# adaLN weights requested ahead of their sums, and differential attention's transposes one stage later, in a decoder block on one core

## The chip, the cores and the metric

The kernel runs on one core of one Trainium2 chip. A core has a matmul engine (TensorE, PE in the profile), three engines for elementwise work (VectorE or DVE, ScalarE or ACT, GpSimd or POOL), a sequencer that issues transfers (SyncE, SP), and 16 DMA engines that bring data from HBM into the core's memory. Matmul results land in eight banks of a separate memory (PSUM), from which DVE and ACT read them. The engines run side by side and wait for one another through semaphores; each works through its own instructions in the order in which they stand in its queue. The metric is the time of one execution on the device, in microseconds (us), as the median of several runs.

## The reference

One decoder block is computed for 512 tokens of width 1024 (cut to what matters here):

```python
mod = jnp.dot(jax.nn.silu(c), w_ada) + b_ada             # w_ada: 1024 x 6144
sh1, sc1, g1, sh2, sc2, g2 = jnp.split(mod, 6, axis=-1)
h = rmsnorm(x, norm_mix) * (1.0 + sc1) + sh1
rq, rk, rv, rg, dq, dk, dv, gate_r, gate_d = jnp.split(jnp.dot(h, w_in), ...)
ro = head_rms(retention(rope(rq), rope(rk), rv)) * jax.nn.silu(rg)      # 4 heads
# differential attention, 4 heads, two softmax maps each, query blocks of 128, causal:
s = jnp.einsum('bqhcd,bkhcd->bhcqk', qi, k) * scale      # c = 0, 1
p = jax.nn.softmax(jnp.where(kpos <= qpos, s, neg), axis=-1)
a = p[:, :, 0] - lam * p[:, :, 1]
o = jnp.einsum('bhqk,bkhe->bqhe', a, v)
do = head_rms(o) * diff_norm * (1.0 - lambda_init)
merged = sigmoid(gate_r) * (ro @ w_ret_o) + sigmoid(gate_d) * (do @ w_diff_o)
x = x + g1 * (merged @ w_out)
y = hierarchical_moe(rmsnorm(x, norm_ffn) * (1.0 + sc2) + sh2, ...)     # 32 experts, 2 per token
x = x + g2 * y;  return rmsnorm(x, norm_final)
```

Only sh1 and sc1 are needed at the start. g1, sh2, sc2 and g2 (four rows of 1024 numbers, each from a slice of w_ada of 1024 x 1024) are needed only behind the mixer.

## The kernel before

**The products that fill TensorE.** The mixer is a sequence of large products of the 512 normalised tokens with slices of 512 columns of `w_in`, `w_ret_o`, `w_diff_o` and `w_out`. Weights arrive in tiles `wst`; ACT rounds each to `whi` (line 179), DVE computes the rest `wlo` (line 180), and each product is three matmuls: high by high, high by low, low by high (`products`, line 225, results in a pool of PSUM banks called `pj`). After every three matmuls `products` calls `tick`, which lets every side job in the list `lanes` advance to its next `yield`. So a side job's instructions stand on PE's queue between product matmuls, and the number of yields between two of its steps says how many threes of product matmuls stand between them. PE's order is the order in which the code is written (`manual_schedule`); on DVE, ACT, POOL and SP a scheduler sets the order when the program is built.

**Side job `ada_rows` (lines 467 to 492).** For each of the four later rows it asks for eight tiles `wa2` of w_ada, 128 x 1024 numbers (512 KB) each (line 474), multiplies each by one column of silu(c) and adds it to `acc` on DVE (lines 476 and 478), yields 6 times after each and 14 times after the last, and then lets PE sum `acc` over the partitions (line 485). `wa2` has two buffers.

**Side job differential attention (`DiffHead`, lines 705 to 760).** It runs in two lanes, each of two heads of four query blocks: eight blocks j = 0 to 7 a lane. The steps of a block are

- `scores` (PE line 724), twice (c = 0, 1), each in a PSUM bank of its own; then on DVE the mask (725), the row maximum (727) and its scaling (728); on ACT the exponential with the row sum (731); on DVE the division and the difference of the two maps (737, 738). A block's scores are 128 x 128, x 256, x 384 or x 512, by the number of keys that its queries see.
- `turn_probs`: PE transposes the probabilities (746), ACT and DVE split them into `aT` and `aTl` (495, 496).
- `values`: PE multiplies them by v (501); ACT squares and sums (535), DVE and POOL make the reciprocal root (536, 537), and DVE scales the result into `od` (757).
- `turn`: two transposes of `od` on PE (572), which ACT and DVE split into `xhi` and `xlo` for the later product with `w_diff_o` (495, 496).

In the text, S(j), Pr(j), V(j) and T(j) are these four steps of block j on PE. `pipelined` (line 576) writes them out: for each block j first T(j-1), then S(j+1), 2 yields, Pr(j), 4 yields, V(j), 4 yields. Retention's heads go through the same function with other numbers.

**The banks.** S (two), Pr, T and V each take a tile of the PSUM pool `pm`, called `ps`, which has three banks and hands them out in turn. A step that writes a bank waits until the step three tiles earlier has been read out.

Of the kernel before, what the change touches and what calls it, by code (L numbers as in the profile page):

```python
# [7 lines left out]
F32 = mybir.dt.float32  # L8
# [5 lines left out]
ALU = mybir.AluOpType  # L14
# [4 lines left out]
P = 128  # L19
D = 1024  # L20
S = 512
KD = D // P
# [19 lines left out]
SIDE_AT = 2, 4, 4, 5  # L42
SIDES = [[(j // 2, j % 2, i) for j in range(4) if SIDE_AT[j] == k for i in range(NT)] for k in range(KD)]
UNITS = [0, 1, 4, 9, 2, 5, 10, 3, 6, 11, 7, 8, 12]
ADA_STEP, ADA_WAIT = 6, 14
RET_WAITS = (4, (2, 5), 2), (3, (4, 6), 2)
DIFF_WAITS = (5, (2, 4, 4), 3), (5, (2, 4, 4), 0)
START_STEPS = (1, 2, 2, 2, 1)
# [85 lines left out]
def block_kernel(tc, a, out):  # L134
    nc = tc.nc
    vec, act, pe, pool = nc.vector, nc.scalar, nc.tensor, nc.gpsimd

    def left(name, bufs=1):
        return open_pool(tc, name, bufs, side="left", reuse_waits="tile")
# [31 lines left out]
    def small(name, cols, dt=F32, p=cp, bufs=None):  # L171
        return p.tile([P, cols], dt, name=name, bufs=bufs)
# [34 lines left out]
    def drain(lane):  # L207
        while lane in lanes:
            tick()
# [21 lines left out]
    def group(pieces, dhi, dlo, transposed, needs=None, kps=()):  # L231

        kps = load_group(pieces, kps)
        banks = new_banks()
        for kp in range(4):
            if kp == 3:
                drain(needs)
            for b in range(4):
                products(banks[b], b, kp, kps[kp], dhi, dlo, transposed)
        return banks  # L240
# [25 lines left out]
    sT = small("sT", KD)  # L266
# [188 lines left out]
    lp, lp_close = left("ada2")  # L455

    def rope(ps, name):
        sw = qk.tile([P, S], F32, name="sw", bufs=2)
        act.copy(sw[0:64, :], ps[64:128, :])
        act.copy(sw[64:128, :], ps[0:64, :])  # L460
        o = qk.tile([P, S], F32, name="qk", bufs=8)
        vec.tensor_mul(o, ps, cosT)
        pool.tensor_mul(sw, sw, sinT)
        vec.tensor_add(o, o, sw)
        return o

    def ada_rows():

        for s_ in range(4):
            lo_col = (2 + s_) * D  # L470
            acc = lp.tile([P, D], F32, name="acc")
            for k in range(KD):
                wa = lp.tile([P, D], F32, name="wa2", bufs=2)
                nc.sync.dma_start(wa, a["w_ada"][0, k * P:(k + 1) * P, lo_col:lo_col + D])
                if k == 0:
                    vec.tensor_scalar(acc, wa, sT[:, 0:1], None, op0=ALU.mult)
                else:
                    vec.scalar_tensor_tensor(acc, wa, sT[:, k:k + 1], acc, op0=ALU.mult, op1=ALU.add)  # L478
                for _ in range(ADA_STEP):
                    yield  # L480
            for _ in range(ADA_WAIT):
                yield
            ps = pm.tile([P, S], F32, name="ps")
            for j in range(4):
                pe.matmul(ps[32 * j:32 * j + 1, 0:256], ones, acc[:, j * 256:(j + 1) * 256], start=True, stop=True)
            brow = lp.tile([P, D], F32, name="wa2", bufs=2)[0:1]
            nc.sync.dma_start(brow, a["b_ada"][:, lo_col:lo_col + D])
            for j in range(4):
                bj = brow[:, j * 256:(j + 1) * 256]
                vec.tensor_add(bj, ps[32 * j:32 * j + 1, 0:256], bj)  # L490
            nc.sync.dma_start(modrow[s_:s_ + 1, :], brow)
            yield

    def split_out(hi, lo, src):
        act.copy(hi, src)
        vec.tensor_sub(lo, src, hi.bitcast(F32))  # L496
# [76 lines left out]
        split_out(hi[:, 2 * h:2 * h + 2, i * P:(i + 1) * P], lo[:, 2 * h:2 * h + 2, i * P:(i + 1) * P],  # L573
                  pt[:, 0:256].rearrange("p (j t) -> p j t", j=2))

    def pipelined(heads, stages, lead, waits, tail):

        blocks = [(head, i) for head in heads for i in range(NT)]
        blocks[0][0].scores(0)
        for _ in range(lead):
            yield
        for j, (head, i) in enumerate(blocks):
            if j:
                p, pi = blocks[j - 1]
                p.turn(pi)
            if j + 1 < len(blocks):
                n, ni = blocks[j + 1]  # L590
                n.scores(ni)
            for stage, wait in zip((None,) + stages, waits):
                if stage:
                    getattr(head, stage)(i)
                for _ in range(wait):
                    yield
        for _ in range(tail):
            yield
        head.turn(i)
# [9 lines left out]
    rolo = hla.tile([P, KD, S], F32R, name="xlo")  # L609
    qkt = [[rope(b, "rq") for b in bs] for bs in (banks[0], banks[1] + [bank])]  # L610
    lanes.append(ada_rows())
    lane = None
    for hp_i in range(2):
        qt, kt = qkt[hp_i][0:2], qkt[hp_i][2:4]
        banks = group([(w_in, 1024 + 512 * hp_i, 512)], hhi, hlo, False, kps=() if hp_i else kps)
        v = [qk.tile([P, NT, 512], F32R, name="v", bufs=4) for _ in range(2)]
        for i in range(NT):
            split_out(v[0][:, i, :], v[1][:, i, :], banks[i])
        banks = group([(w_in, 2048 + 512 * hp_i, 512)], hhi, hlo, False)
        drain(lane)  # L620
        rg2 = rp.tile([P, NT, 512], F32, name="rg2")
        for i in range(NT):
            tg = rp.tile([P, 512], F32, name="tg", bufs=1)
            act.activation(tg, banks[i], AF.Tanh, scale=0.5)
            vec.scalar_tensor_tensor(rg2[:, i, :], tg, 1.0, banks[i], op0=ALU.add, op1=ALU.mult)
        lane = pipelined([RetentionHead(2 * hp_i + j, qt[j], kt[j], v, rg2) for j in range(2)],
                         ("values",), *RET_WAITS[hp_i])
        lanes.append(lane)
# [27 lines left out]
    def second_norm():  # L656
        ps = pm.tile([P, S], F32, name="ps")
        for j in range(4):
            pe.transpose(ps[:, 6 * j:6 * j + 6], block(rows2, j), ident[0:6, 0:6])
        cols2 = ps[:, 0:24].rearrange("p (j s q) -> p j s q", j=4, s=3)  # L660
        sh2v, A2v = [t.rearrange("p (q j) -> p j q", j=4) for t in (sh2, A2)]
        vec.tensor_copy(sh2v, cols2[:, :, 0, :])
        vec.tensor_scalar(A2v, cols2[:, :, 1, :], 1.0, None, op0=ALU.add)
        vec.tensor_mul(A2v, A2v, cols2[:, :, 2, :])
# [97 lines left out]
    for hp_i in range(2):  # L762
        qs, ks = [], []
        for j in range(2):
            h = 2 * hp_i + j
            banks = group([(w_in, 3072 + 256 * h, 256), (w_in, 4096 + 256 * h, 256)], hhi, hlo, True)
            r = [rope(banks[i], "dq") for i in range(4)]
            if h == 0:
                second_norm()
            qs.append(r[0:2])  # L770
            ks.append(r[2:4])
        banks = group([(w_in, 5120 + 512 * hp_i, 512)], hhi, hlo, False)
        drain(lane)
        v = [qk.tile([P, NT, 512], F32R, name="v", bufs=4) for _ in range(2)]
        for i in range(NT):
            split_out(v[0][:, i, :], v[1][:, i, :], banks[i])
        lane = pipelined([DiffHead(2 * hp_i + j, qs[j], ks[j], v) for j in range(2)],
                         ("turn_probs", "values"), *DIFF_WAITS[hp_i])
        lanes.append(lane)

    tgs = [gates(7168, g) for g in range(2)]
# [832 lines left out]
```

## Time and profile before

| | us |
|---|---|
| time, median of 3 runs | 1095.99 (1095.03 to 1098.85) |
| time of the profiled execution | 1092.85 |
| its span in the trace | 1091.0 |
| PE busy | 1040.4 (95%) |
| DVE busy | 623.0 (57%) |
| ACT busy | 339.1 (31%) |
| POOL busy | 77.9 (7%) |

The span is the time from the first to the last instruction in the trace; the time of the same execution lies 1.85 us above it, and the median of the runs 3.14 us above the execution that was profiled. The side job `ada_rows` lies between about 60 and 200 us, lane 0 of differential attention between about 350 and 440 us, lane 1 between about 449 and 528 us; the experts begin at about 612 us.

### The profile page before, as it was taken

The page shows a single profiled execution, that of the slowest core. Times are in us where ns is not written, and L with a number is a line of the kernel's source. Part 1 is how long each engine was busy: PE and PEld are TensorE (multiplying, and loading weights), DVE is VectorE, ACT ScalarE, POOL GpSimd, SP SyncE. Part 2 cuts the span into 40 slices and gives each one's busy share as a digit, 9 for nine tenths or more (in the row PEclk, how much of TensorE's full clock was granted, in tenths as well). Part 3 has the DMA queues.
Part 4 walks back from the last instruction along what each step waited for, and adds up shares of the span by engine and source line. Part 5 has one row for each costly group of instructions (what it writes and reads, how often), then busy time and mean ns, then how long its engine had stood idle before and what let it go on. Part 6 is the DMA issues. An engine that isn't in the chain of part 4 may idle for free.

```text
span 1091.0 us, 14322 instructions
## 1 busy us (share of the span) xinstructions
PE 1040.4 (95%) x5181; PEld 672.1 (62%) x5181; DVE 623.0 (57%) x1452; ACT 339.1 (31%) x701; POOL 77.9 (7%) x103
## 2 busy tenths in 40 slices
PE   5998999999999999999999899999999999999975
PEld 3787788887888776887888644434444344434322
DVE  3368676657445767566666674664565444534344
ACT  4553333333234445344334321111111011111123
POOL 1022000000022022000003300000000000000001
PEclk9999999999999999999999999999999999999988
DMA  9845453535322212225276689999999999999994
GB/s 338 276 155 190 148 184 114 196 116 174 105 89 93 96 43 78 77 77 196 76 247 231 267 345 393 408 393 426 426 427 426 427 426 427 426 426 427 426 427 188
DMA packets 79464, 283.97 MB, mean 260 GB/s; under 512 B 7919, under 2 KB 31503, under 8 KB 54685
## 3 DMA queue, kind: packets, MB, share of 16 engines
q1 hardware_dynamic: 76204, 281.28, 66.2%
q10 hardware_dynamic: 3184, 1.73, 0.6%
q8 instruction: 42, 0.69, 0.2%
q14 instruction: 34, 0.27, 0.1%
HBM read 280.88 MB, written 2.11 MB: 259 GB/s over the span
## 4 chain that ended last, share of the span: by engine, by line
PE 74%; DMA 16%; DVE 5%; ACT 2%; issue 1%; POOL 1%; ACTq 0%; SPq 0%; DVEq 0%; POOLq 0%
PE pj L225 35%; PE gu L1289 12%; DMA ew<-in_w_exp_up_dram 7%; DMA ew<-in_w_exp_down_dram 7%; PE py L1309 6%; PE pa L1060 4%; PE pa L1336 3%; PE pj L407 3%; PE ps L501 2%; PE ps L724 1%; DMA wa<-in_w_ada_dram 1%; PE pt L1299 1%; PE ps L407 1%; DVE acc L478 1%; PE ps L552 1%
## 5 line engine op out<-in xcount | busy, mean ns | idle before, releaser
L1289 PE MATMUL gu<-ew,xT 128*64 128x512 f32 (+1 forms) x1088 | 206.9, 608 | 6.8 <-DMA ew<-in_w_exp_gate_dram 4.2
L225 PE MATMUL pj<-ew,whi 128*128 128x512 f32 x512 | 165.9, 405 | 0.0
L180 DVE TENSOR_TENSOR wlo<-wst,whi 128x1024 fp32r<-128x1024 f32 x79 | 97.4, 1234 | 83.6 <-ACT whi L179 76.6
L225 PE MATMUL pj<-whi,ew 128*128 128x512 f32 x384 | 128.1, 402 | 3.4 <-DVE v L496 3.4
L1289 PEld LDWEIGHTS gu<-ew,xT 128*64 128x64 f32 (+1 forms) x1088 | 52.7, 125 | 114.7 <-issue 92.7
L179 ACT CAST whi<-wst 128x1024 fp32r<-128x1024 f32 x79 | 82.9, 1052 | 123.9 <-PE pj L225 113.7
L1309 PE MATMUL py<-ew,hTm 128*64 128x512 f32 (+1 forms) x544 | 102.7, 608 | 6.4 <-DMA ew<-in_w_exp_down_dram 6.4
L225 PEld LDWEIGHTS pj<-ew,whi 128*128 128x128 f32 x512 | 94.2, 190 | 21.5 <-issue 2.4
L225 PE MATMUL pj<-ew,wlo 128*128 128x512 f32 x256 | 100.6, 393 | 0.0
L225 PEld LDWEIGHTS pj<-whi,ew 128*128 128x128 f32 x384 | 72.8, 190 | 21.3 <-DVE v L496 3.8
L1342 DVE TENSOR_TENSOR x<-x,pa 128x512 f32<-128x512 f32 x96 | 59.5, 681 | 43.6 <-PE pa L1336 43.6
L225 PE MATMUL pj<-wlo,ew 128*128 128x512 f32 x192 | 75.5, 393 | 0.0
L1314 DVE SCALAR_TENSOR_TENSOR yt<-py,ws,g2b 64x512 f32<-64x512 f32 x52 | 39.0, 750 | 59.3 <-PE py L1309 58.5
L1309 PEld LDWEIGHTS py<-ew,hTm 128*64 128x64 f32 (+1 forms) x544 | 27.7, 125 | 69.4 <-issue 52.6
L1294 DVE TENSOR_TENSOR sg<-sg,gu 64x512 f32<-64x512 f32 x26 | 17.9, 690 | 79.7 <-ACT sg L1293 78.8
L225 PEld LDWEIGHTS pj<-ew,wlo 128*128 128x128 f32 x256 | 48.3, 189 | 10.7
L1336 PE MATMUL pa<-xs,ct 128*128 128x512 f32 x196 | 52.3, 407 | 0.1
L1336 PEld LDWEIGHTS pa<-xs,ct 128*128 128x128 f32 x196 | 34.9, 188 | 26.7 <-issue 11.5
L225 PE MATMUL pj<-xhi,whi 128*128 128x512 f32 x128 | 51.0, 399 | 0.0
L225 PE MATMUL pj<-xlo,whi 128*128 128x512 f32 x128 | 50.0, 391 | 0.7 <-DVE xlo L496 0.7
L225 PE MATMUL pj<-xhi,wlo 128*128 128x512 f32 x128 | 49.9, 390 | 0.0
L1330 ACT CAST xs<-yt 128x512 fp32r<-128x512 f32 x25 | 15.5, 618 | 99.7 <-DVE yt L1314 62.5
(366 smaller groups left out, 1568.8 us busy)
## 6 DMA issues: line engine op xcount, KB each, us to landing
ew<-in_w_exp_gate_dram SPq DMA_DIRECT2D x64, 1024.0 KB, 4.7
ew<-in_w_exp_up_dram SPq DMA_DIRECT2D x64, 1024.0 KB, 18.7
ew<-in_w_exp_down_dram SPq DMA_DIRECT2D x64, 1024.0 KB, 19.4
wa<-in_w_ada_dram SPq DMA_DIRECT2D x44, 512.0 KB, 7.4
wst<-in_w_in_dram SPq DMA_DIRECT2D x20, 1024.0 KB, 5.2
wst<-in_w_in_dram SPq DMA_DIRECT2D x16, 512.0 KB, 4.3
wst<-in_w_ret_o_dram SPq DMA_DIRECT2D x4, 1024.0 KB, 4.9
wst<-in_w_diff_o_dram SPq DMA_DIRECT2D x4, 1024.0 KB
```

Of the source, the lines that this page charges most:

```text
L179: act.copy(hi, src[:, off:off + 2, :])
L180: vec.tensor_sub(lo, src[:, off:off + 2, :], hi.bitcast(F32))
L225: pe.matmul(bank, l, r, start=(k == 0 and j == 0), stop=(k == KD - 1 and j == 2))
L407: pe.matmul(bank, w, (hhi, hhi, hlo)[m][:, k, :], start=(k == 0 and m == 0), stop=(k == KD - 1 and m == 2))
L501: pe.matmul(out, l[a_], r[b_], start=start and j == 0, stop=stop and j == 2)
L1060: pe.matmul(ps, self.G[:, i, :], hx[:, i, ns], start=(i == 0 and j == 0), stop=(i == NT - 1 and j == 1))
L1289: pe.matmul(self.gu[r:r + n, :], self.g.xT[:, k, c:c + n], w[name, k // 4][:, k % 4, :], start=(k == 0), stop=(k == KD - 1))
L1294: vec.tensor_mul(self.sg, self.sg, self.gu[64:P, :])
L1309: pe.matmul(py[r:r + n, :], self.hT[:, k, n * q:n * q + n], w[k // 2][:, 2 * (k % 2) + nh, :], start=(k == 0), stop=(k == 3))
L1314: vec.scalar_tensor_tensor(yt[r, ns], py[64 * nh:64 * nh + 64, :], self.g.w[r], g2b[r, ns], op0=ALU.mult, op1=ALU.mult)
L1336: pe.matmul(po, self.ct[:, i * P:(i + 1) * P], self.ys[nh][:, j, :], start=start and j == 0, stop=(j == 1))
L1342: vec.tensor_add(x1[:, i, ns], x1[:, i, ns], po)
```

## The change

`ada_rows`: each tile `wa2` is requested one pass of the loop before its sum is written. A pass is 6 yields, so tile k+1 is requested, 6 yields pass, and then the sum of tile k is written. A ninth pass takes the last sum; the wait behind the loop falls from 14 to 8 yields, so 62 yields pass per row, as before. The number of buffers stays two.

Differential attention, both lanes: T(j-1) no longer stands at the head of block j but behind Pr(j). The yields are unchanged, as are retention and the last T of a lane.

```diff
-ADA_STEP, ADA_WAIT = 6, 14
+ADA_STEP, ADA_WAIT = 6, 8
...
-            for k in range(KD):
-                wa = lp.tile([P, D], F32, name="wa2", bufs=2)
-                nc.sync.dma_start(wa, a["w_ada"][0, k * P:(k + 1) * P, lo_col:lo_col + D])
-                if k == 0:
-                    vec.tensor_scalar(acc, wa, sT[:, 0:1], None, op0=ALU.mult)
-                else:
-                    vec.scalar_tensor_tensor(acc, wa, sT[:, k:k + 1], acc, op0=ALU.mult, op1=ALU.add)
+            ahead = []
+            for k in range(KD + 1):
+                if k < KD:
+                    wa = lp.tile([P, D], F32, name="wa2", bufs=2)
+                    nc.sync.dma_start(wa, a["w_ada"][0, k * P:(k + 1) * P, lo_col:lo_col + D])
+                    ahead.append((k, wa))
                 for _ in range(ADA_STEP):
                     yield
+                if len(ahead) > 1 or k == KD:
+                    at, wa = ahead.pop(0)
+                    if at == 0:
+                        vec.tensor_scalar(acc, wa, sT[:, 0:1], None, op0=ALU.mult)
+                    else:
+                        vec.scalar_tensor_tensor(acc, wa, sT[:, at:at + 1], acc, op0=ALU.mult, op1=ALU.add)
...
-            if j:
+            if j and not late:
                 p, pi = blocks[j - 1]
                 p.turn(pi)
...
-            for stage, wait in zip((None,) + stages, waits):
+            for at, (stage, wait) in enumerate(zip((None,) + stages, waits)):
                 if stage:
                     getattr(head, stage)(i)
+                if j and at == 1 and late:
+                    p, pi = blocks[j - 1]
+                    p.turn(pi)
...
-                         ("turn_probs", "values"), *DIFF_WAITS[hp_i])
+                         ("turn_probs", "values"), *DIFF_WAITS[hp_i], late=True)
```

The lines below these move down by 5 to 9: line 478 of before is 485 after, 496 is 501, 572 is 577, 724 is 733, 731 is 740, 746 is 755.

**PE, lane 1, block 1.** First before, then after. `od` is the block's output, `qk` the queries and keys, `pt` the probabilities; the rows of `pj` are product matmuls.

```order
L225 MATMUL pj<-ew_117,wlo 128x512
L572 MATMUL ps<-cst,od 128x128 x2
L724 MATMUL ps<-qk 128x384 x2
L225 MATMUL pj<-ew_118,whi 128x512
...
L225 MATMUL pj<-ew_118,wlo 128x512
L746 MATMUL ps<-cst,pt 128x128 x2
L225 MATMUL pj<-ew_118,whi 128x512
```

```order
L225 MATMUL pj<-ew_117,wlo 128x512
L733 MATMUL ps<-qk 128x384 x2
L225 MATMUL pj<-ew_118,whi 128x512
...
L225 MATMUL pj<-ew_118,wlo 128x512
L755 MATMUL ps<-cst,pt 128x128 x2
L577 MATMUL ps<-cst,od 128x128 x2
L225 MATMUL pj<-ew_118,whi 128x512
```

The two transposes of `od` stood ahead of the scores of the next block; they stand now behind the transposes of the probabilities, with six product matmuls between the scores and them. On PE this is all that moves in the program, seven times in each lane.

**DVE, at about 100 us.** First before, then after. `acc` is the sum of `ada_rows`, `wlo` the low half of a weight, `v` retention's values, split out of the product banks `pj`.

```order
L180 TENSOR_TENSOR wlo<-wst,whi 128x1024
L478 SCALAR_TENSOR_TENSOR acc<-wa_803,sT,acc 128x1024
L180 TENSOR_TENSOR wlo<-wst,whi 128x1024
L478 SCALAR_TENSOR_TENSOR acc<-wa_824,sT,acc 128x1024
L496 TENSOR_TENSOR v<-pj,v 128x512 x3
L478 SCALAR_TENSOR_TENSOR acc<-wa_879,sT,acc 128x1024
L496 TENSOR_TENSOR v<-pj,v 128x512
```

```order
L180 TENSOR_TENSOR wlo<-wst,whi 128x1024
L485 SCALAR_TENSOR_TENSOR acc<-wa_802,sT,acc 128x1024
L180 TENSOR_TENSOR wlo<-wst,whi 128x1024
L501 TENSOR_TENSOR v<-pj,v 128x512
L485 SCALAR_TENSOR_TENSOR acc<-wa_823,sT,acc 128x1024
L501 TENSOR_TENSOR v<-pj,v 128x512 x2
L485 SCALAR_TENSOR_TENSOR acc<-wa_878,sT,acc 128x1024
L501 TENSOR_TENSOR v<-pj,v 128x512
```

One split of `v` moved ahead of one sum; the first sum and the low half behind it stay ahead of all of them.

**DVE, lane 0, scores of block 7 (128 x 512).** First before, then after. `qk` at lines 462 and 464 is the rotation of the next queries and keys, `mx` the row maximum of the scores.

```order
L757 SCALAR_TENSOR_TENSOR od<-ps,s_3393,dnb 128x256
L180 TENSOR_TENSOR wlo<-wst,whi 128x1024
L496 TENSOR_TENSOR xlo<-ps,xhi 128x2x128
L462 TENSOR_TENSOR qk<-pj,cosT 128x512 x2
L464 TENSOR_TENSOR qk<-qk,sw 128x512 x2
L725 TENSOR_TENSOR ps<-ps,maskneg 128x128 x2
L727 TENSOR_REDUCE mx<-ps 128x1
L462 TENSOR_TENSOR qk<-pj,cosT 128x512 x2
L464 TENSOR_TENSOR qk<-qk,sw 128x512 x2
L728 TENSOR_SCALAR mx<-mx 128x1
```

```order
L766 SCALAR_TENSOR_TENSOR od<-ps,s_3393,dnb 128x256
L180 TENSOR_TENSOR wlo<-wst,whi 128x1024
L462 TENSOR_TENSOR qk<-pj,cosT 128x512 x2
L464 TENSOR_TENSOR qk<-qk,sw 128x512 x2
L734 TENSOR_TENSOR ps<-ps,maskneg 128x128 x2
L736 TENSOR_REDUCE mx<-ps 128x1
L462 TENSOR_TENSOR qk<-pj,cosT 128x512 x2
L464 TENSOR_TENSOR qk<-qk,sw 128x512 x2
L737 TENSOR_SCALAR mx<-mx 128x1
```

Only the split of the transposes (`xlo`) has left its place; the two pairs of rotations still stand between the first map's maximum and its scaling.

## Rows read from the trace of the kernel before

**Rows 1.** Windows (us from the span's start): length, busy by engine (PE, PEld, DVE, ACT, POOL), PEclk, DMA, GB/s.

```profile
608.00:612.00 4.00, 3.49 (x18) 2.62 (x19) 1.01 (x8) 2.77 (x9) 1.61 (x2) 1.00 0.00 0
612.00:1071.00 459.00, 442.28 (x2319) 192.18 (x2317) 237.54 (x642) 77.71 (x165) 3.14 (x5) 0.98 0.99 415
```

**Rows 2.** PE's waits, 90 to 530 us: line waited for, us in total, times, longest.

```profile
PE pj L225 <- DVE v L496: 3.4, 1, 3.4
PE ps L572 <- DVE od L757: 2.5, 2, 2.2
PE ps L501 <- DVE aTl L496: 2.4, 1, 2.4
...
PE ps L572 <- DVE ro L564: 0.6, 1, 0.6
```

**Rows 3.** Timeline, DVE and PE, 99 to 104 us: start, length, instruction, [idle before <-releaser].

```profile
99.08 1.28 DVE L478 SCALAR_TENSOR_TENSOR acc<-wa,sT,acc 128x1024 f32<-128x1024 f32 x1 [2.79 <-DMA wa<-in_w_ada_dram]
100.29 1.22 DVE L180 TENSOR_TENSOR wlo<-wst,whi 128x1024 fp32r<-128x1024 f32 x1
101.42 1.28 DVE L478 SCALAR_TENSOR_TENSOR acc<-wa,sT,acc 128x1024 f32<-128x1024 f32 x1
102.62 1.88 DVE L496 TENSOR_TENSOR v<-pj,v 128x512 fp32r<-128x512 f32 x3
...
103.35 0.80 PE L225 MATMUL pj<-whi,ew 128*128 128x512 f32 x1 [3.38 <-DVE v L496]
```

**Rows 4.** Windows of 4 us behind the three longest PE waits, columns as in rows 1.

```profile
104.00:108.00 4.00, 4.00 (x14) 3.18 (x13) 3.42 (x4) 0.00 (x0) 0.00 (x0) 0.68 0.87 289
...
388.00:392.00 4.00, 2.64 (x11) 2.28 (x12) 3.56 (x7) 0.37 (x1) 1.93 (x2) 0.73 0.00 0
392.00:396.00 4.00, 4.00 (x19) 3.25 (x18) 2.04 (x11) 2.13 (x5) 0.00 (x0) 0.84 0.00 0
...
428.00:432.00 4.00, 3.90 (x21) 3.39 (x22) 2.96 (x10) 1.18 (x4) 0.55 (x1) 1.00 0.40 103
```

**Rows 5.** Timeline, DVE, the sum ahead of `ro` at 134 us.

```profile
134.20 1.28 DVE L478 SCALAR_TENSOR_TENSOR acc<-wa,sT,acc 128x1024 f32<-128x1024 f32 x1
```

**Rows 6.** Timeline, lane 1, block 1 (scores 128x384): PE, ACT.

```profile
460.86 0.39 PE L572 MATMUL ps<-cst,od 128*128 128x128 f32 x2
461.08 1.46 PE L724 MATMUL ps<-qk 128*128 128x384 f32 x4
463.76 0.38 PE L746 MATMUL ps<-cst,pt 128*128 128x128 f32 x2
...
464.18 0.37 ACT L495 CAST aT<-ps 128x256 fp32r<-128x256 f32 x1 [2.04 <-PE ps L746]
464.88 0.58 ACT L731 ACTIVATE pt<-ps,mx 128x384 f32<-128x384 f32 x1 [0.33 <-DVE mx L728]
```

**Rows 7.** Timeline, lane 1, block 2 (scores 128x512): PE, ACT.

```profile
473.53 0.49 PE L746 MATMUL ps<-cst,pt 128*128 128x128 f32 x3
...
472.96 0.69 ACT L731 ACTIVATE pt<-ps,mx 128x512 f32<-128x512 f32 x1 [1.69 <-DVE mx L728]
```

**Rows 8.** Timeline, lane 0, block 3 (scores 128x128): PE, DVE.

```profile
396.20 0.40 PE L501 MATMUL ps<-v,aT 128*128 128x256 f32 x2
...
388.73 0.48 DVE L757 SCALAR_TENSOR_TENSOR od<-ps,s,dnb 128x256 f32<-128x256 f32 x1 [0.44 <-POOL s L537]
...
391.33 0.68 DVE L464 TENSOR_TENSOR qk<-qk,sw 128x512 f32<-128x512 f32 x1
391.93 0.48 DVE L725 TENSOR_TENSOR ps<-ps,maskneg 128x128 f32<-128x128 f32 x2
```

**Rows 9.** Timeline, lane 0, block 6 (scores 128x512): PE, ACT.

```profile
422.19 0.49 PE L746 MATMUL ps<-cst,pt 128*128 128x128 f32 x3
428.10 0.51 PE L501 MATMUL ps<-v,aT 128*128 128x256 f32 x2 [2.36 <-DVE aTl L496]
...
427.01 0.69 ACT L731 ACTIVATE pt<-ps,mx 128x512 f32<-128x512 f32 x1 [0.20 <-DVE mx L728]
```

More of the change, by code (lines that the diff above doesn't have):

```diff
@@ L574, in turn_out, with pipelined @@
                   pt[:, 0:256].rearrange("p (j t) -> p j t", j=2))
-    def pipelined(heads, stages, lead, waits, tail):
+    def pipelined(heads, stages, lead, waits, tail, late=False):
         blocks = [(head, i) for head in heads for i in range(NT)]
```

## Prediction

> **What bounds the kernel now.** I first asked which part of the span turns a delay into time. From 612 us on, DMA is busy for 0.99 of the time and the experts live on weights as they arrive; in the 4 us ahead of that, DMA is idle (share 0.00) and TensorE works alone [rows 1]. So the end is a DMA stretch of fixed length, and its start hangs on TensorE. Up to there PE is nearly always busy, and whatever it waits more or less moves the end about one to one.
>
> Second, PE's waits between 90 and 530 us, where both edits lie. There are few: 3.4 us for a split of v, 2.5 us in two pieces for `od` ahead of T, 2.4 us for `aTl` ahead of V, 0.6 us for retention's `ro` [rows 2]. Together they are under 10 us, which is all that better placing can win directly.
>
> Third, the granted clock behind the longer waits. The 3.38 us wait at 103 us is followed by 0.68 of full clock, the 2.2 us wait at 389 us by 0.73 and 0.84, but the 2.36 us wait at 428 us by 1.00 [rows 3, 4, 9]. Of the two levels, 1.2 and 2.4 GHz, the shares below 1.00 mean that part of the window ran at the lower. The loss is (1 - 0.68) x 4 = 1.3 us at 104, and (0.27 + 0.16) x 4 = 1.7 us at 388. An idle PE can thus cost up to 1.7 us beyond its idling, and need not.
>
> **The change, `ada_rows`.** Amount of work, transfers and buffers stay. With two `wa2` buffers, the request of tile k+2 still waits until sum k has read its buffer, so a request can't get further ahead than one sum. The DVE sequence decides. At 99 us DVE waits 2.79 us for a tile, sums (1.28 us), makes a `wlo` (1.22 us), sums again (1.28 us), and only then splits v, for which PE stands still for 3.38 us [rows 3]. After, the wait, the first sum and the `wlo` stay ahead; one split passes the second sum. PE starts 102.62 - 101.42 = 1.2 us earlier. If the shorter idling leaves the clock up, 1.3 us more come back; then PE reaches the second bank after six matmuls, while its split stands behind the sum, which takes back up to 0.45 us (split 0.63, sum 1.2, split 0.63 against 1.37 for six matmuls at full clock, an estimate from rows 3). The gain is 1.2 to 2.1 us; I take 1.6. At 136 us `ro` passes a sum (1.28) and a `wlo`, and PE's 0.6 us wait goes [rows 2, 5]: 0.6. The sums that move to later places meet no waiting PE in the trace: 0, and up to 0.5 us if one lands ahead of a rotation. Sum: -2.2 us (-2.7 to -1.2).
>
> **The change, T behind Pr.** Nothing is added. What moves is what T waits for. Before, it waited for `od` and a bank read out long ago. After, tiles go round as S, S, Pr, T, V on three banks, so T(j-1) takes the bank of the first map of S(j+1), written only six product matmuls earlier. It must wait until ACT has read that map in its exponential, behind DVE's mask, maximum and scaling. PE's queue is in order, so the products behind T wait too.
>
> The Trainium skill, page "Perfetto Trace Analysis", section "Optimizing Tensor Performance", asks that independent matmul groups rotate through different banks, so that reading one out overlaps the next group. The rule speaks against this place: T meets a bank just filled. If T always met one already read out, the new waits would be zero and the sum that of the rival named Faster, below; rows 6 to 9 tell block by block.
>
> *Scores of 384 keys* (blocks 1 and 5 of each lane). Without T ahead, S and Pr start 0.22 us earlier (461.08 - 460.86), so T's place is at 463.76. The exponential ended at 464.88 + 0.58 = 465.46 [rows 6]. DVE no longer splits `xlo` ahead of the mask, which gives back about 0.4; ACT still reads out `aT` first. So T starts near 465.0: a new wait of 1.2 us (0.9 to 1.7) where PE had none. Three such blocks (the fourth is counted below): +3.6 us (2.7 to 5.1).
>
> *Scores of 512 keys, lane 1.* The exponential ends at 473.65; T's place is 473.53 - 0.22 + 0.36 = 473.67 [rows 7]. No wait, and likewise for 128 and 256 keys, whose maxima are shorter: +0.2 us for all. In lane 0, block 2 has the rotations of the next heads between its maxima on DVE; between no wait [rows 7] and 1.2 us [rows 6] I take 0.7.
>
> *Lane 0, block 3.* Here the old wait was: T(2) stood 2.2 us for `od`, with S(4) behind it [rows 2]. After, S(4) goes ahead, but Pr(3) needs the bank of V(2), which `od` reads until 389.21, and T(2) needs the exponential of S(4). On DVE `od` is followed by a rotation's product, mask, its sum, maximum and scaling: 0.68 + 0.24 + 0.68, and some 0.4 for the two last (an estimate from the mask, which reads as much), about 2.0 us, then an exponential of at most 0.58 [rows 6, 8]. T starts at 391.8, or 392.6 if a rotation waits for POOL. From T to V are two transposes and twelve matmuls, about 3.1 us (an estimate: in block 6, Pr's three transposes and as many matmuls took 428.10 - 2.36 - 422.19 = 3.55 [rows 9]). V(3) comes at 394.9 to 395.7 against 396.20 [rows 8] at full clock, and up to 1.7 later with the old dip. I take -0.2 us (-1.4 to +1.2).
>
> *Lane 0, blocks 5 and 6.* S(7) has 512 keys, and on DVE two pairs of rotations stand ahead of the scaling for its first exponential, after as before (the order shows it). That exponential ended at 427.70, T(5)'s place is near 422.8 [rows 9]: PE, which worked on until 425.74, now stands from 422.8 to about 427.7. The old 2.36 us wait of V(6) vanishes behind it, but twelve matmuls that lay ahead of it now come after: V(6) at 427.7 + 3.1 = 430.8 against 428.10. That is +2.7 us. Block 5's own wait starts this later, and the missing `xlo` and the other 0.3 us wait for `od` starts it earlier; I take +2.7 for both blocks (2.3 to 3.9).
>
> Sum: -2.2 + 3.6 + 0.2 + 0.7 - 0.2 + 2.7 = +4.8 us. On the profiled execution (1092.85) that is 1097.7; on the median, 3.14 us above it, 1095.99 + 4.8 = 1100.8.
>
> **The rivals.** *The clock falls* behind the new waits of block 3 and block 6 of lane 0, as it did at 388 us: 1.7 us each, up to 1104 to 1106. For it: the longest new wait (4.9 us) is longer than any that the trace has. Against it: 428 us [rows 4]. The Trainium skill says on the page "Perfetto Trace Analysis", section "Matmul Optimizations", that the engine scales power by utilization, so matmuls should run back to back; by it the sum would be 3.4 us higher, and rows 4 agree in two of three cases.
>
> *Balance.* All waits at their cheap ends: -2.7 + 2.7 + 0 - 1.4 + 2.3 = +0.9, about 1097. For it: the pieces hang on tenths of a microsecond between engines.
>
> *Faster.* The exponentials are always in time, because DVE, rid of `xlo`, reaches the masks earlier, and S no longer waits for `od`. Then the removals stand alone: 2.7 + 2.2 + 1.7 + 0.3 = 6.9 us, about 1089. It decides where the new waits stay under 6.9 - 3.3 = 3.6 us. Against it: rows 6 have the exponential 1.7 us behind T's place, and rows 9 by 4.9, and no freed DVE instruction is as long.
>
> *`ada_rows` doesn't do what it says.* The scheduler, not the text, orders DVE, and two buffers hold the requests back; if the splits gain nothing, the time is 1103.
>
> **How the numbers follow.** Forecast with waits as worked out, 0.45; clock falls, 0.15; no gain in `ada_rows`, 0.03; balance, 0.26; faster, 0.11. About 0.3% (3.3 us) is what a measurement of this kernel can tell from no change. So: faster 0.11, same 0.26, slower 0.63. The predicted time is 1100.8; the ends of the terms and the clock give 1094 to 1106.
>
> **What would show it.** In the profile after: PE waits of the transposes (L577) for ACT (L740), about 1.2 us in blocks 1 and 5 of both lanes, one of 4 to 5 us near 425 us; no wait for `od` at T and none for `aTl` at V; PE's wait for v near 2.2 us, none for `ro`; the experts' start 4 to 5 us later. Wrong would be the forecast if the exponentials end ahead of the transposes, or if the experts start no later though PE waited more.

## The result

The changed kernel takes 1100.74 us (median of 19 runs, 1098.30 to 1107.36) against 1095.10 us of the kernel before on the same chip (19 runs, 1091.56 to 1098.85): a ratio of 1.0058 with a 95% interval of 1.0046 to 1.0071, 5.6 us slower. The profiled execution has a span of 1098.6 us, 7.6 us above that of before. Most executions of one kernel lie within 3 us of its median, and the profiled one of before (1092.85) is 2.3 us below it, that of the changed kernel (1100.37) 0.4; so the difference of two profiles shows where time goes, and the medians show how much.

PE's waits of the changed kernel between 60 and 540 us (columns as in rows 2), to be read against [rows 2]:

```profile
PE ps L577 <- ACT pt L740: 11.4, 7, 5.1
PE pj L225 <- DVE v L501: 2.0, 1, 2.0
PE ps L577 <- DVE ro L569: 1.3, 2, 1.0
PE pj L225 <- DVE xlo L501: 0.4, 1, 0.4
```

The first line is new: in seven blocks the moved transposes (line 577) wait for ACT's exponential (line 740), 11.4 us in sum. The waits for `od` and for `aTl`, 4.9 us, are gone. The wait for v has shrunk by 1.3 us, from 3.38 to 2.05, and that for retention's `ro` has grown by 0.7. In sum PE's waits grew from 9.6 to 15.1 us, by 5.5, and between 60 and 612 us the clock fell twice in either trace (at 104 and 388 us before, at 104 and 428 us after).

How much of this reaches the end is seen by taking the same PE instruction in both traces. The table gives how much later it starts after than before (us; worked out from the timelines of PE, the moved transposes left out). It counts from 99 us, ahead of the first wait, where the changed kernel's PE is 0.23 us later from the span's start.

| stretch of the kernel before | later by, at its end | change in the stretch |
|---|---|---|
| to 112 us: split of v | -1.07 | -1.1 |
| to 137 us: `ro` at 137 | -1.85 | -0.8 |
| to 152 us: the next two `ro` | -0.19 | +1.7 |
| to 358 us | -0.58 | -0.4 |
| lane 0, block 1 (384 keys) | +0.68 | +1.3 |
| lane 0, block 2 (512 keys) | +1.21 | +0.5 |
| lane 0, block 3 | -0.76 | -2.0 |
| lane 0, blocks 4 and 5 | +0.67 | +1.4 |
| lane 0, blocks 6 and 7 | +4.03 | +3.4 |
| lane 1, block 1 (384 keys) | +5.26 | +1.2 |
| lane 1, blocks 2 to 4 | +5.23 | 0.0 |
| lane 1, block 5 (384 keys) | +6.49 | +1.3 |
| to 611 us | +7.01 | +0.5 |
| end of the span | +7.36 | +0.3 |

From 611 us on nothing is won back: the experts begin 7 us later, and the end comes as much later and 0.3 us more. Here the windows of the changed kernel that answer to [rows 1] (columns as there), two windows of 4 us later, with DMA again at 0.99 from there on:

```profile
616.00:620.00 4.00, 4.00 (x21) 2.98 (x20) 1.25 (x4) 2.08 (x8) 2.36 (x2) 1.00 0.17 33
620.00:1079.00 459.00, 441.32 (x2315) 191.53 (x2313) 236.97 (x642) 77.84 (x165) 2.40 (x5) 0.98 0.99 415
```

Lane 1, block 1, the places of [rows 6]; timeline of PE, then of ACT:

```profile
467.81 0.38 PE L755 MATMUL ps<-cst,pt 128*128 128x128 f32 x2
469.22 0.44 PE L577 MATMUL ps<-cst,od 128*128 128x128 f32 x2 [1.04 <-ACT pt L740]
472.25 0.40 PE L506 MATMUL ps<-v,aT 128*128 128x256 f32 x2
...
468.22 0.37 ACT L500 CAST aT<-ps 128x256 fp32r<-128x256 f32 x1 [2.08 <-PE ps L755]
468.49 0.59 ACT L740 ACTIVATE pt<-ps,mx 128x384 f32<-128x384 f32 x1
```

The transposes' place is behind those of the probabilities, at 468.0; ACT first reads out `aT`, then the scores until 469.08, and PE starts at 469.22. The product matmuls behind it on PE's queue stand with it.

Lane 0, block 6, the places of [rows 9]; timeline of PE, then of ACT, then windows:

```profile
422.44 0.49 PE L755 MATMUL ps<-cst,pt 128*128 128x128 f32 x3
427.99 0.69 PE L577 MATMUL ps<-cst,od 128*128 128x128 f32 x2 [5.07 <-ACT pt L740]
432.55 0.40 PE L506 MATMUL ps<-v,aT 128*128 128x256 f32 x2
...
427.16 0.69 ACT L740 ACTIVATE pt<-ps,mx 128x512 f32<-128x512 f32 x1 [2.17 <-DVE mx L737]
```

```profile
424.00:428.00 4.00, 0.01 (x1) 0.01 (x1) 3.71 (x7) 1.74 (x4) 1.92 (x2) 0.98 0.00 0
428.00:432.00 4.00, 4.00 (x12) 3.29 (x13) 2.10 (x8) 1.04 (x3) 0.00 (x0) 0.59 0.00 0
```

PE does nothing for a whole window while DVE is busy for 3.71 of its 4 us, mostly with the rotations that stand ahead of the scaling; the exponential ends at 427.85 and the transposes start at 427.99. Then the granted clock is 0.59 of full speed, which costs (1 - 0.59) x 4 = 1.6 us more.

### The profile page after: what moved, and what is told of

Same layout as the page of the kernel before. It is cut to its first block, busy times and chain, and to the rows that moved or that the text cites. A ratio compares the mean times of both kernels' runs of the same rounds, so it can differ in the third digit from the quotient of the medians.

```text
span 1098.6 us, 14307 instructions
## 1 busy us (share of the span) xinstructions
PE 1040.9 (95%) x5181; PEld 671.4 (61%) x5181; DVE 623.3 (57%) x1452; ACT 338.9 (31%) x701; POOL 76.9 (7%) x103
## 4 chain that ended last, share of the span: by engine, by line
PE 72%; DMA 17%; DVE 6%; issue 2%; ACT 2%; POOL 1%; SPq 0%; DVEq 0%; ACTq 0%; POOLq 0%
PE pj L225 34%; PE gu L1298 12%; DMA ew<-in_w_exp_up_dram 7%; DMA ew<-in_w_exp_down_dram 7%; PE py L1318 6%; PE pa L1069 4%; PE pa L1345 3%; PE pj L407 3%; PE ps L506 2%; DMA wa<-in_w_ada_dram 2%; PE ps L733 1%; DVE acc L485 1%; PE pt L1308 1%; PE ps L407 1%; DVE qk L464 1%
```

## The experiments

All ratios are to the kernel before, run on the same chip.

**1. `ada_rows` alone.** The changed loop over the weights stays; the lanes are called without the later transposes:

```
-                         ("turn_probs", "values"), *DIFF_WAITS[hp_i], late=True)
+                         ("turn_probs", "values"), *DIFF_WAITS[hp_i])
```

> The ada_rows part alone; the transposes stay at the head of the block. Theory (the sums' order moves PE's waits about, but the weights come no earlier with two buffers): PE waits about 2.0 us for v at 102 us (3.4 before), but 1.3 us for retention's ro behind sums that wait for their weights (0.6 before); net between 0 and -1 us, a ratio of 0.999 to 1.000 to the kernel before. Rival (the prediction's term): -2.2 us, a ratio of 0.998.

Measured: 1.0008 (0.9989 to 1.0026). Nothing that can be told from no change; the rival's 0.998 lies outside. PE's longest waits in its profile:

```profile
PE ps L577 <- DVE ro L569: 3.4, 2, 3.0
PE ps L577 <- DVE od L766: 2.5, 2, 2.2
PE ps L506 <- DVE aTl L501: 2.4, 1, 2.4
PE pj L225 <- DVE v L501: 2.3, 1, 2.3
```

The wait for v is shorter by 1.1 us than in [rows 2], but that for `ro` is longer by 2.8, not by the 0.7 expected. The changed kernel has the same at a smaller size; first its timeline of DVE and the PE row that waits, then the same two of this kernel:

```profile
145.70 2.60 DVE L485 SCALAR_TENSOR_TENSOR acc<-wa,sT,acc 128x1024 f32<-128x1024 f32 x2 [1.76 <-DMA wa<-in_w_ada_dram]
148.23 0.15 DVE L541 TENSOR_SCALAR s<-s 128x1 f32<-128x1 f32 x1
149.03 0.48 DVE L569 SCALAR_TENSOR_TENSOR ro<-ps,s,rg 128x256 f32<-128x256 f32 x1 [0.66 <-POOL s L542]
...
149.66 0.41 PE L577 MATMUL ps<-cst,ro 128*128 128x128 f32 x2 [1.02 <-DVE ro L569]
```

```profile
146.94 2.60 DVE L485 SCALAR_TENSOR_TENSOR acc<-wa,sT,acc 128x1024 f32<-128x1024 f32 x2 [3.69 <-DMA wa<-in_w_ada_dram]
...
150.90 0.41 PE L577 MATMUL ps<-cst,ro 128*128 128x128 f32 x2 [2.96 <-DVE ro L569]
```

Two sums stand ahead of the steps to `ro`, and in the changed kernel they wait 1.76 us for their weights. PE, which comes 1.4 us earlier than before, stops for them. In this kernel's execution the sums waited 3.69 us, 1.9 us longer, hence PE's 2.96.

**2. The later transposes alone.** `ada_rows` as before, with `ADA_WAIT` 14:

```
-            ahead = []
-            for k in range(KD + 1):
...
+            for k in range(KD):
+                wa = lp.tile([P, D], F32, name="wa2", bufs=2)
```

> The later transposes alone, with ada_rows as before. Theory: all of the loss is here; seven PE waits of the transposes for ACT's exponential, 11 us in sum, less the old waits for od and aTl that vanish: +6 to +7.5 us, a ratio of 1.0055 to 1.007 to the kernel before. Rival (the two parts hurt each other, by moving DVE's work in the same places): +4 us or less here, and a loss in the ada_rows part alone.

Measured: 1.0057 (1.0037 to 1.0078), as much as the whole change (1.0058). PE's wait for the exponential is the same:

```profile
PE ps L572 <- ACT pt L735: 11.4, 7, 5.1
```

The same reckoning as in the table gives +1.3, +0.5, -2.0, +1.4 and +3.1 us for the stretches of lane 0 and +1.2 and +1.3 for the two blocks of lane 1. The loss is in the transposes, and no effect of one part on the other is seen within these intervals.

**3. The transposes another two yields later.**

```
-                if j and at == 1 and late:
-                    p, pi = blocks[j - 1]
-                    p.turn(pi)
-                for _ in range(wait):
+                for n_ in range(wait):
+                    if j and at == 1 and late and n_ == 2:
+                        p, pi = blocks[j - 1]
+                        p.turn(pi)
                     yield
```

> The changed kernel with each moved pair of transposes another two yields (six product matmuls, 1.37 us) later, halfway between the probabilities' transposes and values. Theory (the cost is that the scores' bank isn't read out yet, by 0.5 to 1.5 us in most blocks and 5 us in one): the waits of 0.5 to 1.5 us go to zero, that of 5.1 us falls to about 3.7; 6 to 7 us come back against the changed kernel, a time near 1094, a ratio of 0.998 to 1.000 to the kernel before. Rival (transposes placed late cost by themselves, or the falling clock is what costs): no more than 2 us come back, a ratio of 1.004 or more.

Measured: 1.0010 (0.9994 to 1.0027). About 5 us come back by six matmuls' distance, of the 6 to 7 expected. PE's waits for the exponential:

```profile
PE ps L577 <- ACT pt L740: 5.1, 2, 3.7
```

Five of the seven waits are gone, the longest fell from 5.07 to 3.69, by the 1.37 us that six matmuls take. So the later place by itself isn't what costs; being handed a bank that isn't read out is. Most of what keeps the time from falling below that of before is block 6: by the table's reckoning this kernel loses 2.4 us there.

**4. One block.** The kernel before, with the transposes later in block 3 of lane 0 alone (`late` is there a block's number):

```
-            if j and not late:
+            if j and j != late:
...
-                if j and at == 1 and late:
+                if j and at == 1 and j == late:
...
-                         ("turn_probs", "values"), *DIFF_WAITS[hp_i], late=True)
+                         ("turn_probs", "values"), *DIFF_WAITS[hp_i], late=(3, 0)[hp_i])
```

> The kernel before with the transposes moved in one block alone, block 3 of lane 0, where PE waited 2.2 us for od and the clock then fell. Theory: this block gains what the changed kernel's trace shows there, 2.0 us, and nothing else moves: -2 us, a ratio of 0.998. Rival (the gain there came from the blocks ahead, which were later in the changed kernel): no gain, 1.000, or a loss of 1 to 2 us from the new wait.

Measured: 1.0022 (1.0007 to 1.0036), slower, against the theory; the rival had a loss of 1 to 2 us. Block 3 costs 1.3 us by the table's reckoning here, where it gained 2.0 in the changed kernel. First the rows of the changed kernel, then those of this one (PE, DVE, ACT):

```profile
390.25 0.62 PE L755 MATMUL ps<-cst,pt 128*128 128x128 f32 x4
392.63 0.44 PE L577 MATMUL ps<-cst,od 128*128 128x128 f32 x2 [1.76 <-ACT pt L740]
...
387.36 0.68 DVE L464 TENSOR_TENSOR qk<-qk,sw 128x512 f32<-128x512 f32 x1
...
389.68 0.48 DVE L766 SCALAR_TENSOR_TENSOR od<-ps,s,dnb 128x256 f32<-128x256 f32 x1 [0.44 <-POOL s L542]
...
392.12 0.37 ACT L740 ACTIVATE pt<-ps,mx 128x128 f32<-128x128 f32 x1 [3.84 <-DVE mx L737]
```

```profile
391.12 0.66 PE L750 MATMUL ps<-cst,pt 128*128 128x128 f32 x4 [0.27 <-DVE od L761]
394.74 0.44 PE L572 MATMUL ps<-cst,od 128*128 128x128 f32 x2 [2.97 <-ACT pt L735]
...
390.58 0.48 DVE L761 SCALAR_TENSOR_TENSOR od<-ps,s,dnb 128x256 f32<-128x256 f32 x1 [0.44 <-POOL s L537]
390.98 1.35 DVE L464 TENSOR_TENSOR qk<-qk,sw 128x512 f32<-128x512 f32 x1
...
394.23 0.37 ACT L735 ACTIVATE pt<-ps,mx 128x128 f32<-128x128 f32 x1 [1.83 <-DVE mx L732]
```

The same edit in the same block met another DVE order: here, as in the kernel before, a rotation's sum (line 464, 1.35 us) stands between `od` and the mask of the scores; in the changed kernel it stood ahead of `od`. From the end of `od` to the end of the exponential it is 3.54 us here and 2.33 there, 1.21 us more, and by as much PE's wait is longer, 2.97 us against 1.76. Behind it the clock fell. A window of this kernel, and then one of the changed one, show it:

```profile
396.00:400.00 4.00, 4.00 (x15) 3.17 (x15) 1.53 (x3) 1.04 (x1) 0.00 (x0) 0.61 0.00 0
```

```profile
392.00:396.00 4.00, 3.37 (x17) 2.84 (x18) 3.09 (x12) 2.61 (x7) 0.00 (x0) 1.00 0.00 0
```

Block 3's gain in the changed kernel is thus a shorter wait, owed to the order that the scheduler found for the whole, and a clock that stayed up behind it.

**5. Three buffers for `ada_rows`,** alone, in its changed form:

```
-                    wa = lp.tile([P, D], F32, name="wa2", bufs=2)
+                    wa = lp.tile([P, D], F32, name="wa2", bufs=3)
...
-            brow = lp.tile([P, D], F32, name="wa2", bufs=2)[0:1]
+            brow = lp.tile([P, D], F32, name="wa2", bufs=3)[0:1]
```

The lanes are called as in experiment 1.

> The ada_rows part alone, with three buffers for the weights instead of two, so that a request really can stand two sums ahead. Theory (two buffers hold the requests back; the part alone moved nothing): DVE's waits of the sums for their weights shrink from 15 us to under 5, the split of v comes 2 us or more earlier, PE's waits for v and ro, 5.7 us in the part alone, fall to about 1; -2 to -4 us, a ratio of 0.996 to 0.998 to the kernel before. Rival (the transfers themselves are late because other weights are ahead of them on the queue, buffers don't matter): 0.999 to 1.001, and the DVE waits stay.

Measured: 0.9974 (0.9958 to 0.9990), against 1.0008 with two buffers. DVE's waits for the weights, PE's waits for v and `ro`, and the sums ahead of the split of v on DVE:

```profile
DVE acc L485 <- DMA wa<-in_w_ada_dram: 8.6, 7, 1.9
```

```profile
PE pj L225 <- DVE v L501: 2.4, 1, 2.4
...
PE ps L577 <- DVE ro L569: 1.8, 3, 1.1
```

```profile
96.66 1.28 DVE L485 SCALAR_TENSOR_TENSOR acc<-wa,sT,acc 128x1024 f32<-128x1024 f32 x1
99.80 1.28 DVE L485 SCALAR_TENSOR_TENSOR acc<-wa,sT,acc 128x1024 f32<-128x1024 f32 x1 [1.86 <-DMA wa<-in_w_ada_dram]
```

DVE's waits fall from 17.4 us in experiment 1 (15.3 in the changed kernel) to 8.6, so the buffers did hold the requests back. But PE's waits for v and `ro` fell only from 5.7 to 4.2 us, not to about 1: with the requests earlier, one more sum (96.66) stands ahead of the split of v, and the last one there still waits 1.86 us. The kernel got faster by the ratio, but the profiled execution is the slowest of its twelve (1096.18 us, median 1092.22), so it doesn't show where, and that stays open.

**6. The transposes just ahead of those of the probabilities,** instead of just behind them:

```
+                if j and at == 1 and late:
+                    p, pi = blocks[j - 1]
+                    p.turn(pi)
                 if stage:
                     getattr(head, stage)(i)
-                if j and at == 1 and late:
-                    p, pi = blocks[j - 1]
-                    p.turn(pi)
```

> The changed kernel with the moved transposes just ahead of those of the probabilities instead of just behind them; the transposes then take the bank of the last values, and the probabilities' transposes take the bank of the first scores. Theory (whoever is handed the bank of the scores six matmuls later waits for the exponential): PE's waits for ACT's exponential, 11 us in seven, now stand at the probabilities' transposes, and the time stays that of the changed kernel or a little worse, a ratio of 1.005 to 1.007 to the kernel before. Rival (the transposes of od wait for their own data or are late by their place): the waits vanish, a ratio of 1.000.

Measured: 1.0091 (1.0062 to 1.0119), slower than the range expected. PE's waits for the exponential, and then the row of block 3 from its timeline:

```profile
PE ps L755 <- ACT pt L740: 13.0, 7, 5.2
```

```profile
393.64 1.12 PE L755 MATMUL ps<-cst,pt 128*128 128x128 f32 x4 [3.11 <-ACT pt L740]
```

The seven waits have changed their line: it is now the probabilities' transposes (755) that are handed the bank of the scores, and they wait. The transposes of `od` wait for nothing. This settles that the bank's turn is the cause, and not what `od`'s transposes need themselves. Block 3 waits 3.11 us here instead of 1.76, and behind it the clock fell to 0.62; by the table's reckoning it costs 0.6 us where it gained 2.0 in the changed kernel.

**7. Two yields later, but not in block 6 of lane 0,** with `ada_rows` as before: experiment 3's edit and

```
-            if j and not late:
+            if j and (not late or j in late[1]):
...
+                    if j and at == 1 and late and n_ == 2 and j not in late[1]:
...
+                         ("turn_probs", "values"), *DIFF_WAITS[hp_i], late=(True, ((6,), ())[hp_i]))
```

> ada_rows as before; transposes two yields behind those of the probabilities, but at the head of the block, as before, in block 6 of lane 0, whose exponential comes behind two pairs of rotations on DVE. Theory: no wait for the exponential but about 1.4 us in block 3, the clock stays up there, block 6 waits 2.4 us as before: -2 us, a ratio of 0.998 to the kernel before. Rival (block 6's loss isn't due to its place but to all that is late ahead of it): +1 us, 1.001.

Measured: 0.9978 (0.9964 to 0.9992), faster than the kernel before and 0.8% faster than the changed one, as the theory had it. PE's waits in the two lanes:

```profile
PE ps L501 <- DVE aTl L496: 2.4, 1, 2.4
PE ps L572 <- ACT pt L735: 1.4, 1, 1.4
...
PE ps L572 <- DVE od L761: 0.3, 1, 0.3
```

What is left of the exponential is 1.4 us in block 3; block 6 waits for `aTl` as before. Against experiment 3 this is 0.3%, or 3.5 us, for the place of two transposes in one block and the old `ada_rows`, whose part experiment 1 could not tell from nothing.

**8. Experiment 7's transposes and experiment 5's buffers together.**

> The last but one and the last but two together: the changed ada_rows with three buffers, and the transposes two yields later but in block 6 of lane 0. Theory: the two gains add up, -4 to -6 us, a ratio of 0.9945 to 0.9965 to the kernel before. Rival (either gain is noise of the clock and of the transfers): 0.998 or more.

Measured: 0.9972 (0.9955 to 0.9989), at 1092.20 us with experiment 5 (1092.22) the lowest, but not the sum of the two (0.9952), and between the theory's range and the rival's. The interval doesn't exclude 0.996, nor that the buffers add nothing.

## Why the prediction held, and where not

The direction, the size and the mechanism came out: +4.8 us forecast, +5.6 measured, a time of 1100.8 forecast and 1100.74 measured. That the last two nearly coincide is luck twice over. The forecast stood on a median of 3 runs, 1095.99, that 19 runs put 0.9 us lower. And three terms of the sum were off, one of them the other way, so that they cancelled in part: in the pair of profiles they come to 1.9 us more than forecast, while the medians rose by 0.8 more.

- *What bounds the kernel.* Right. The shift at 611 us is the shift at the end but for 0.3 us, and PE's waits, 5.5 us more than before, are the most of it.
- *Blocks of 384 keys.* Right: 1.2 us each forecast for three of them; +1.3, +1.2 and +1.3 measured. The fourth is block 5 of lane 0, below. The waits themselves are 1.0 to 1.2 us, and the transposes behind them take a little longer than in a stream.
- *Lane 1's other blocks, and block 2 of lane 0.* Right: +0.2 and +0.7 forecast, 0.0 and +0.5 measured.
- *`ada_rows`.* The term was mis-sized: -2.2 us forecast, -0.6 in the profile and nothing by experiment 1's ratio. Its first half held (-1.1 at the split of v, where the clock fell again, to 0.62, behind a wait of 2.05 us, so that none of the 1.3 us came back; -0.8 at 137 us). The step that failed is "The sums that move to later places meet no waiting PE in the trace: 0, and up to 0.5 us": two steps of `ro` further on, sums that wait for their weights met it, and took back 1.7 us. A PE that comes earlier by 1.9 us meets waits that it didn't meet before, because the weights come no earlier: DVE's waits for them are 14.8 us before and 15.3 after. The sentence ahead of it, that two buffers hold the requests back, was the one to draw this from.
- *Block 3 of lane 0.* Mis-sized: -0.2 us forecast (-1.4 to +1.2), -2.0 measured. The mechanism was as told (a short wait for the exponential in place of that for `od`), but the wait of 1.76 us left the clock at 1.00 [rows 4 have 0.73 and 0.84 there], and I had put about half of that dip into the value. Besides, the waits of blocks 1 and 2 had made PE 1.2 us later at the head of this block, and `od` only 0.7 later (389.68 against 388.73, less the 0.23 from which the table counts): where PE waited for DVE before, part of an earlier delay is absorbed, and the sum added the blocks as if none were. Experiment 4 shows the other way it can go: 2.97 us of waiting and 0.61.
- *Blocks 5 and 6.* Mis-sized: +2.7 us forecast (2.3 to 3.9), +4.8 measured (1.4 and 3.4). PE's wait of 5.07 us was forecast at 4.9, V(6) forecast 2.7 later came 432.55 - 428.10 = 4.45 later. Of the 2.1 us that were missing, 1.6 is the clock at 0.59, and 0.3 that the exponential ended late enough for the transposes to start at 427.99 and not 427.7. The prediction had the clock as the rival "the clock falls", at 0.15. For this block it was likelier than that: behind the waits of 5.07 us here and in experiment 2 and of 5.2 us in experiment 6 the clock fell each time.
- *The rivals.* "Balance" and "Faster" fell with the 11.4 us of waits. "The clock falls" held in block 6 and not in block 3. That `ada_rows` doesn't do what it says held too, at 0.03, by experiment 1, and experiment 5 bears out its reason, that two buffers hold the requests back: the 2.2 us that the sum had there did not come.

The rule of the Trainium skill, page "Perfetto Trace Analysis", section "Optimizing Tensor Performance", to rotate independent matmul groups through different banks so that reading out overlaps, is borne out here with 11.4 us of waits where a rotation of three banks brought a group to a bank still being read, and 13.0 us when another group was brought there.

## What to carry to other kernels

When a step is moved along an engine's queue, ask which buffer it is then handed, not only what data it needs: in a rotation of few banks each step inherits the reader of the bank's last owner, and a place that looks free can wait for work started moments before. Such a place is found by walking the rotation through the new order and comparing, block by block, when the reader ends with when the step comes; six matmuls (1.37 us) of distance took 11.4 us of waits down to 5.1 here, and one block left out of it to 1.4, at the price of the old wait of 2.4 us in that block. A request written earlier in the code got its data earlier here only with a buffer free for it.

Not tried: a fourth bank for `pm`, taken from the five of `pj`. By the rotation the moved transposes would then get the bank of V(j-1), which is read out once `od`, their own input, is there; what the other steps and `pj` would lose or gain no run shows.

## What the runs showed of the hardware

The granted clock behind a wait of PE differed between executions for waits of middling length. In these profiles, the waits of 1.76 us and shorter in block 3 (1.76 in the changed kernel, 1.44 in experiment 3) left it at 1.00; waits of 2.97, 3.38, 3.69 and 5.07 us were followed by windows of 0.61, 0.68, 0.62 and 0.59. Between them it went either way: the wait of 2.05 us for v in the changed kernel was followed by 0.62, that of 2.96 us for `ro` in experiment 1 by 1.00, and the wait of 2.36 us for `aTl` in block 6, the same within 0.01 us in six profiles, by 1.00 in three (the kernel before, experiments 4 and 8) and by less in three (1, 5 and 7). The first window is that of the changed kernel behind its wait for v, the second experiment 1's behind the wait for `ro`, the two others experiment 1's behind the wait for `aTl`:

```profile
104.00:108.00 4.00, 4.00 (x12) 3.21 (x12) 3.52 (x4) 0.00 (x0) 0.00 (x0) 0.62 0.81 226
```

```profile
152.00:156.00 4.00, 4.00 (x25) 3.51 (x23) 4.00 (x6) 1.45 (x4) 0.00 (x0) 1.00 0.24 97
```

```profile
428.00:432.00 4.00, 2.72 (x11) 2.62 (x12) 2.95 (x8) 1.22 (x6) 0.00 (x0) 0.68 0.13 29
432.00:436.00 4.00, 4.00 (x18) 3.18 (x18) 2.02 (x6) 1.11 (x4) 0.55 (x1) 0.89 0.68 235
```

So the same wait cost (0.32 + 0.11) x 4 = 1.7 us more in one execution than in another. Which way it goes no run here tells ahead. In the 29 runs of the kernel before that stand beside experiments 5 to 8, the fastest (1090.66 us) has a mean granted clock of 0.992 and the slowest (1098.02 us) of 0.981, so the clock goes with the spread between executions of one kernel; how much of the spread it makes is not shown. At this size medians of a dozen runs decide, and not a pair of profiles.
